# A two-block network in fp32 on one core: another order of the first loads, gated values in the temporaries' tag, mLSTM denominators by a unit column, its maxima in float32r, and a last store in two parts

## The chip, the cores and the metric

The kernel runs on one core of a Trainium2 chip, as one launch. The metric is device time in microseconds. Engines are named as in the profile: PE is TensorE's matmuls, PEld its weight loads, DVE is VectorE, ACT ScalarE, POOL GpSimd, SP the engine that issues most DMAs. A small q behind a name is that engine's sequencer.

## What is computed

A sequence of 256 rows of width 1024 goes through two blocks. The first has a SwiGLU feed-forward, a hybrid mixer (a Fourier branch and differential attention with a T5 bias by 32 distance buckets), a second SwiGLU and a norm. The second has an mLSTM mixer, a SwiGLU, causal attention with rotary positions (one block of 256, so no selected blocks), and a SwiGLU. Cut to what matters:

```python
def swiglu(x, wg, wu, wd):
    return (jax.nn.silu(x @ wg) * (x @ wu)) @ wd
...
# mLSTM, in chunks of 64, carried state c, n, m
m_t = jnp.maximum(inter, jnp.max(dmat, axis=-1))
w_intra = jnp.exp(dmat - m_t[..., None])
qk = jnp.einsum('bhtd,bhsd->bhts', qc, kc) * w_intra
num = jnp.einsum('bhts,bhsv->bhtv', qk, vc) + w_inter[..., None] * jnp.einsum('bhvd,bhtd->bhtv', c_st, qc)
den = jnp.sum(qk, axis=-1) + w_inter * jnp.einsum('bhd,bhtd->bht', n_st, qc)
h_out = num / jnp.maximum(jnp.abs(den), jnp.exp(-m_t))[..., None]
```

All weights and activations are fp32.

## The kernel before

**Pieces.** All large products run through one routine, `products`. Weights are cut into pieces of 128 x 1024 (512 KB): two row blocks of 128 by 512 columns. There are 376 pieces, laid out in the order of use by `make_plan`. A piece is split into a high part in float32r (`whi`, cast by ScalarE, L173) and the remainder (`wlo`, subtracted by VectorE, L236); activations are split in the same way. Each piece then takes 12 matmuls of 128 x 512: high weights by high and by low activations (L450, L451) and low weights by high activations (L448), into two PSUM banks, one for each half of the 256 rows. In this text pieces are counted from 0; a chunk is the pieces that add into one pair of banks. The first feed-forward (44 pieces up, 11 chunks of 4) takes its first three chunks interleaved, so pieces 0 to 11 are chunks 0 to 2 and end with pieces 9, 10 and 11; chunk 3 is pieces 12 to 15 and chunk 4 pieces 16 to 19. In the last piece of a chunk the low weights come after four matmuls, otherwise after eight.

**Order.** The schedule is written out by hand. `products` gives a piece's matmuls and then calls `step`. `step` runs what was put down for this step ahead of the pump (`pre`), the pump, what was put down for after it (`post`), and then at most a few background jobs, for which each step earns a credit. The pump of step s issues the load of piece s + 9 on SP (L159), the ScalarE cast of piece s + 4 and the VectorE remainder of piece s + 3. There are six raw buffers, six for `whi` and six for `wlo`: the load of piece k needs the remainder of piece k - 6 to be done, and the cast of piece k the matmuls of piece k - 6. Every engine works through its own instructions in order, SP through its loads too; a load also waits for the landing of one issued eight loads before.

**The start.** `start` issues the small constants on ScalarE's queue and all else on SP: the transposed input in four pairs of blocks (`xt`, 256 KB each), pieces 0 to 3, tables, and the four tiles of x (256 KB each). It splits pieces 0 to 2 itself. The rest of the constants (762 KB with gains and biases, `pos` 130 KB, tables 320 KB, gates 32 KB) is issued in `run` at step 3 (L1188 to L1191).

**A chunk's evacuation in a feed-forward** (`ffn`). One step after a chunk's last piece, `evac` writes silu(gate) with ScalarE (L501) and multiplies the other half in with VectorE (L502), in a tile with the tag g (four buffers). `turn_far` transposes it in blocks (L329), writes it to DRAM a step later (L338), reads it back turned three steps later (L335), and five steps later `split_far` splits it (L347, L348). The tile g, its transposed copy and the tile read back all have the tag g.

**Background jobs** (`t5_jobs`). They make the T5 bias during the first feed-forward: prepare (from `pos`, L517 to L521), distance, sides, least (four values into the bias and the first two values by ScalarE, L549), and then 30 copies: each has ScalarE write the two values for the next copy and VectorE copy two values into the bias where a bucket's mask holds (L564). The temporaries have the tag t2 (five buffers). The earliest place of prepare is the end of step 9; that of least is the end of step 15.

**The mLSTM** (`mlstm`). For 256 rows the recurrence is done in one piece for each of the four heads. `gates2b` scans the running maximum `mr` (4 x 256). `decay(h)` broadcasts head h's row of it over 128 partitions by a matmul with a selector, in fp32 (L881, K = 4), and makes the weights. `score(h)` multiplies the scores in (L892, L893). `numer(h)` multiplies by v (L909) and, for the denominator, by a column of ones (L911), both in fp32, where one matmul runs as two passes in the trace; it does so for the first half of rows with one product and for the second with two. ScalarE copies the result out and squares it (L913, L915). After the last numerator the output gate's sigmoid needs a table load (L794), then VectorE gates head 0 (L935) and TensorE transposes it (L308).

**The end.** `residual` adds the last sums to x and stores each 128 x 512 tile from SP (L473, L477).

Of the kernel before, what the change touches and what calls it, by code (L numbers as in the profile page):

```python
# [12 lines left out]
F32 = mybir.dt.float32  # L13
F32R = mybir.dt.float32r
# [8 lines left out]
P = 128  # L23
S = 256
D = 1024
KB = D // P
# [64 lines left out]
class Net:  # L91
# [89 lines left out]
    def start(self):  # L181

        nc, a = self.nc, self.a
        raw = [self.raw(i) for i in range(4)]
        xt = [self.slot() for _ in range(KB // 2)]

        def part(q, i, c0=0, c1=1024):
            o = self.plan[i][2]
            q.dma_start(raw[i][:, c0:c1], self.plan[i][1][:, o + c0:o + c1])

        def load_xt(q, i):
            q.dma_start(xt[i].rearrange("p (b t) -> p b t", b=2), a["xt"][2 * i:2 * i + 2].rearrange("b p t -> p b t"))

        nc.scalar.dma_start(self.cst[:, :C_AG], a["cst"][:, :C_AG])
        load_xt(nc.sync, 0)
        part(nc.sync, 0, 0, 512)
        part(nc.sync, 0, 512)
        part(nc.sync, 1)
        part(nc.sync, 2)
        load_xt(nc.sync, 1)  # L200
        part(nc.sync, 3)
        load_xt(nc.sync, 2)
        load_xt(nc.sync, 3)
        nc.sync.dma_start(self.tbl[:, :T_CMASK], a["tbl"][:, :T_CMASK])
        for c in range(2):
            for tb in range(2):
                nc.sync.dma_start(self.x[c][tb], a["x"][tb * P:(tb + 1) * P, c * 512:(c + 1) * 512])
        self.loaded = 4
# [18 lines left out]
        self.cast = 3  # L227
        for n in range(2, KB):
            self.later(max(0, n // 2 - 2), lambda n=n: split_x(n)(), post=n > 3)
# [235 lines left out]
    def residual(self, st, scale=None, gain=None, out=None):  # L465
# [3 lines left out]
        def f(c, acc):  # L469
            for tb in range(2):  # L470
# [5 lines left out]
                if out is not None:  # L476
                    nc.sync.dma_start(out[tb * P:(tb + 1) * P, c * 512:(c + 1) * 512], x)  # L477
            if st is not None and gain is None:
                self.norm_half(st, c, self.x[c])
            elif st is not None:  # L480
# [12 lines left out]
    def ffn(self, st, up, dn, res, slack=(0.0, 0.0), cross=(2, 2)):  # L493
# [3 lines left out]
        def evac(f, acc):  # L497
            ht = self.tp.tile([P, 2, S], F32, name="g", tag="g", bufs=4)
# [12 lines left out]
    def t5_jobs(self):  # L511
# [22 lines left out]
        def sides():  # L534
# [5 lines left out]
            self.bias = self.cp.tile([P, 4, 2 * S], F32, name="t5bias")  # L540

        def least():
            for h in range(4):
                value(0, h, self.bias[:, h])
            lay(1, 0)
# [11 lines left out]
        def copy(b, i):  # L557
# [5 lines left out]
            for j in range(2):  # L563
                nc.vector.copy_predicated(self.bias[:, 2 * i + j], T["m"], v[j])  # L564
# [204 lines left out]
    def mlstm(self, st, res):  # L769
# [7 lines left out]
        sel = self.slot()  # L777
# [526 lines left out]
```

## Time and profile before

| | |
|---|---|
| median of 3 runs | 1111.71 us (1111.59 to 1113.0) |
| the profiled execution's own time | 1112.17 us |
| its span, first to last instruction | 1110.4 us |
| busy: PE, PEld, DVE, ACT | 99%, 82%, 66%, 56% |
| bytes moved by DMA | 226 MB, 204 GB/s in the mean |
| granted TensorE clock, mean | 1.00 |

How to read it: the time is that of the profiled run, the span what the trace covers. Matmuls are pipelined, so PE's busy share says that matmuls follow each other, not that each runs at its peak; a lost microsecond is seen where the start of a matmul is late, not in the share. The rows further below are from that one execution.

### The profile page before, as it was taken

The page shows a single profiled execution, that of the slowest core. Times are in us where ns is not written, and L with a number is a line of the kernel's source. Part 1 is how long each engine was busy: PE and PEld are TensorE (multiplying, and loading weights), DVE is VectorE, ACT ScalarE, POOL GpSimd, SP SyncE. Part 2 cuts the span into 40 slices and gives each one's busy share as a digit, 9 for nine tenths or more (in the row PEclk, how much of TensorE's full clock was granted, in tenths as well). Part 3 has the DMA queues.
Part 4 walks back from the last instruction along what each step waited for, and adds up shares of the span by engine and source line. Part 5 has one row for each costly group of instructions (what it writes and reads, how often), then busy time and mean ns, then how long its engine had stood idle before and what let it go on. Part 6 is the DMA issues. An engine that isn't in the chain of part 4 may idle for free.

```text
span 1110.4 us, 14227 instructions
## 1 busy us (share of the span) xinstructions
PE 1099.4 (99%) x5034; PEld 909.2 (82%) x5034; DVE 727.7 (66%) x1136; ACT 620.2 (56%) x927; POOL 24.6 (2%) x27
## 2 busy tenths in 40 slices
PE   8999999999999999999999999999999999999998
PEld 7878888878888888888877888888888888888887
DVE  5689998475685665645654677756558865665752
ACT  6497876666645554535645564545445665554541
POOL 0000000000000000000001000000003000000000
PEclk9999999999999999999999999999999999999999
DMA  9788876543555877766443556877455445777760
GB/s 319 271 242 245 256 237 205 190 151 112 193 173 166 255 230 258 225 210 209 155 130 113 191 187 212 282 251 268 156 173 180 147 151 182 245 233 247 241 229 29
DMA packets 89583, 226.19 MB, mean 204 GB/s; under 512 B 10148, under 2 KB 34340, under 8 KB 89512
## 3 DMA queue, kind: packets, MB, share of 16 engines
q1 hardware_dynamic: 88928, 224.86, 62.7%
q8 instruction: 39, 0.64, 0.2%
q10 hardware_dynamic: 584, 0.44, 0.2%
q14 instruction: 32, 0.26, 0.1%
HBM read 212.67 MB, written 12.58 MB: 203 GB/s over the span
## 4 chain that ended last, share of the span: by engine, by line
PE 94%; DMA 2%; DVE 2%; ACT 1%; issue 1%; SPq 1%; DVEq 0%; ACTq 0%
PE acc L450 29%; PE acc L448 29%; PE acc L451 29%; DMA wraw<-f_up 2%; PE acc L308 2%; DVE wlo L236 1%; PE acc L909 1%; PE acc L616 0%; PE acc L661 0%; SPq L335 0%; PE acc L1053 0%; PE acc L702 0%; PE acc L1079 0%; PE acc L1111 0%; DVE g L502 0%
## 5 line engine op out<-in xcount | busy, mean ns | idle before, releaser
L236 DVE TENSOR_TENSOR wlo<-wraw,whi 128x1024 fp32r<-128x1024 f32 x373 | 441.2, 1214 | 47.8 <-ACT whi L173 47.6
L173 ACT ACTIVATE whi<-wraw 128x1024 fp32r<-128x1024 f32 x373 | 381.2, 1053 | 108.6 <-PE acc L451 76.8
L450 PE MATMUL acc<-whi,xs 128*128 128x512 f32 x1024 | 404.4, 395 | 2.3 <-ACT whi L224 1.4
L451 PE MATMUL acc<-whi,xs 128*128 128x512 f32 x1024 | 399.0, 390 | 0.0
L448 PE MATMUL acc<-wlo,xs 128*128 128x512 f32 x1024 | 284.7, 389 | 2.7 <-DVE wlo L236 2.7
L450 PEld LDWEIGHTS acc<-whi,xs 128*128 128x128 f32 x1024 | 192.2, 188 | 44.6 <-issue 2.7
L448 PEld LDWEIGHTS acc<-wlo,xs 128*128 128x128 f32 x1024 | 192.1, 188 | 43.8 <-DVE wlo L236 3.6
L451 PEld LDWEIGHTS acc<-whi,xs 128*128 128x128 f32 x1024 | 192.4, 188 | 38.7
L450 PE MATMUL acc<-whi,h 128*128 128x512 f32 x480 | 187.9, 391 | 0.0
L451 PE MATMUL acc<-whi,h 128*128 128x512 f32 x480 | 186.8, 389 | 0.0
L448 PE MATMUL acc<-wlo,h 128*128 128x512 f32 x480 | 131.3, 389 | 0.0
L502 DVE SCALAR_TENSOR_TENSOR g<-acc,rsqn,g 128x256 f32<-128x256 f32 x88 | 40.9, 480 | 112.1 <-ACT g L501 111.4
L448 PEld LDWEIGHTS acc<-wlo,h 128*128 128x128 f32 x480 | 90.1, 188 | 18.8
L451 PEld LDWEIGHTS acc<-whi,h 128*128 128x128 f32 x480 | 90.2, 188 | 18.4
L450 PEld LDWEIGHTS acc<-whi,h 128*128 128x128 f32 x480 | 90.1, 188 | 18.3
L501 ACT ACTIVATE g<-acc,rsqn 128x256 f32<-128x256 f32 x88 | 39.8, 471 | 110.1 <-PE acc L448 109.3
L347 ACT ACTIVATE h<-g 128x512 fp32r<-128x512 f32 x44 | 27.6, 628 | 47.6 <-DMA g<-far 47.4
L292 ACT ACTIVATE xs<-acc,cst 128x256 fp32r<-128x256 f32 x48 | 21.5, 473 | 56.2 <-PE acc L308 42.7
L348 DVE TENSOR_TENSOR h<-g,h 128x512 fp32r<-128x512 f32 x44 | 30.2, 686 | 31.1 <-ACT h L347 31.1
L549 ACT ACTIVATE t<-side,cst 128x512 f32<-128x512 bf16 x60 | 45.4, 802 | 1.6 <-DVE t5bias L564 1.6
L473 DVE TENSOR_TENSOR x<-acc,x 128x512 f32<-128x512 f32 x20 | 13.5, 688 | 45.7 <-PE acc L448 45.7
L564 DVE COPY_PREDICATED t5bias<-t5m,t 128x512 f32<-128x512 uint8 x60 | 41.3, 743 | 0.5
(222 smaller groups left out, 525.5 us busy)
## 6 DMA issues: line engine op xcount, KB each, us to landing
wraw<-g_up SPq DMA_DIRECT2D x88, 512.0 KB, 5.0
wraw<-f_up SPq DMA_DIRECT2D x87, 512.0 KB, 5.3
wraw<-f_dn SPq DMA_DIRECT2D x44, 512.0 KB, 4.3
wraw<-g_dn SPq DMA_DIRECT2D x44, 512.0 KB, 4.4
wraw<-w_in SPq DMA_DIRECT2D x32, 512.0 KB, 4.1
wraw<-a_w_in SPq DMA_DIRECT2D x24, 512.0 KB, 4.5
wraw<-b_w_in SPq DMA_DIRECT2D x24, 512.0 KB, 4.8
far<-g SPq DMA_DIRECT2D x44, 256.0 KB, 4.4
```

Source lines behind the costliest of these rows:

```text
L173: nc.scalar.activation(wh[:, :m], raw[:, :m], AF.Copy)
L236: self.nc.vector.tensor_sub(wl[:, :m], raw[:, :m], self.pieces[i][1][:, :m].bitcast(F32))
L308: self.nc.tensor.transpose(pt[:, o:o + P], src[tb][:, j * P:(j + 1) * P], self.ident)
L347: nc.scalar.activation(to(hi), src, AF.Copy)
L348: nc.vector.tensor_sub(to(lo), src, to(hi).bitcast(F32))
L448: nc.tensor.matmul(acc[tb], xh, w[kk][1], start=False, stop=last and kk == 1)
L450: nc.tensor.matmul(acc[tb], xh, w[kk][0], start=k == 0, stop=False)
L451: nc.tensor.matmul(acc[tb], xl, w[kk][0], start=False, stop=False)
L501: nc.scalar.activation(ht[:, tb], acc[tb][:, :S], AF.Silu, scale=r)
L502: nc.vector.scalar_tensor_tensor(ht[:, tb], acc[tb][:, S:], r, ht[:, tb], ALU.mult, ALU.mult)
L549: nc.scalar.activation(dst, T["side"], AF.Identity, bias=self.cst[:, c:c + 1], scale=self.cst[:, c + 64:c + 65])
L564: nc.vector.copy_predicated(self.bias[:, 2 * i + j], T["m"], v[j])
```

## The change

It does five things. `start` issues the loads in another order: eight constants and the first block of the transposed input on ScalarE's queue; on SP the first half of piece 0, the second block, and then pieces 0 to 5 with the other blocks between, then x tiles alternating with pieces 6 to 8, and the constants behind them. The warm-up matmuls follow the loads in the program and are nine instead of ten. The splits of the other blocks, the squares of x, the norm and the rest of the constants move to later steps (the constants from step 3 to step 6). The gated tile in `ffn` takes its buffer from the tag t2 instead of g. In the mLSTM, v lies in the T5 bias's memory (free by then, 257 wide for each head), with a column of ones, so that the numerator's matmul gives the denominator in column 256; the running maxima are split in two float32r halves and broadcast by two float32r matmuls. The last tile is added and stored in two halves, the second from ScalarE's queue.

```diff
 
     def start(self):
...
         nc, a = self.nc, self.a
-        raw = [self.raw(i) for i in range(4)]
+        raw = {}
         xt = [self.slot() for _ in range(KB // 2)]
 
-        def part(q, i, c0=0, c1=1024):
+        def part(i, c0=0, c1=1024):
+            if i not in raw:
+                raw[i] = self.raw(i)
             o = self.plan[i][2]
-            q.dma_start(raw[i][:, c0:c1], self.plan[i][1][:, o + c0:o + c1])
-
-        def load_xt(q, i):
-            q.dma_start(xt[i].rearrange("p (b t) -> p b t", b=2), a["xt"][2 * i:2 * i + 2].rearrange("b p t -> p b t"))
-
-        nc.scalar.dma_start(self.cst[:, :C_AG], a["cst"][:, :C_AG])
-        load_xt(nc.sync, 0)
-        part(nc.sync, 0, 0, 512)
-        part(nc.sync, 0, 512)
-        part(nc.sync, 1)
-        part(nc.sync, 2)
+            nc.sync.dma_start(raw[i][:, c0:c1], self.plan[i][1][:, o + c0:o + c1])
+            self.loaded = i + 1
+
+        def load_xt(q, n, m=1):
+            o = n % 2 * S
+            q.dma_start(xt[n // 2][:, o:o + m * S].rearrange("p (b t) -> p b t", b=m),
+                        a["xt"][n:n + m].rearrange("b p t -> p b t"))
+
+        def load_x(c, tb):
+            nc.sync.dma_start(self.x[c][tb], a["x"][tb * P:(tb + 1) * P, c * 512:(c + 1) * 512])
+
+        nc.scalar.dma_start(self.cst[:, :KB], a["cst"][:, :KB])
+        load_xt(nc.scalar, 0)
+        part(0, 0, 512)
         load_xt(nc.sync, 1)
-        part(nc.sync, 3)
-        load_xt(nc.sync, 2)
-        load_xt(nc.sync, 3)
-        nc.sync.dma_start(self.tbl[:, :T_CMASK], a["tbl"][:, :T_CMASK])
-        for c in range(2):
-            for tb in range(2):
-                nc.sync.dma_start(self.x[c][tb], a["x"][tb * P:(tb + 1) * P, c * 512:(c + 1) * 512])
-        self.loaded = 4
+        part(0, 512)
+        part(1)
+        part(2)
+        load_xt(nc.sync, 2, 2)
+        part(3)
+        part(4)
+        load_xt(nc.sync, 4, 2)
+        part(5)
+        load_xt(nc.sync, 6, 2)
+        load_x(0, 0)
+
+        z = self.tmp("sq")
+        nc.vector.memset(z, 0.0)
+        nc.scalar.activation(self.tmp("sq")[:, :8], z[:, :8], AF.Copy)
+        junk = self.bank()
+        for _ in range(9):
+            nc.tensor.matmul(junk[:, :P], z[:, :P], z[:, P:], start=True, stop=True)
         xs = [self.xsp.tile([P, 2, S], F32R, name="xs", tag="xs") for _ in range(KB)]
 
         def split_x(n):
                 lo()
                 nc.vector.tensor_sub(w[1][:, c], raw[i][:, c], w[0][:, c].bitcast(F32))
         self.cast = 3
+        for i, c, tb in ((6, 0, 1), (7, 1, 0), (8, 1, 1)):
+            part(i)
+            load_x(c, tb)
+        nc.sync.dma_start(self.cst[:, KB:C_AG], a["cst"][:, KB:C_AG])
+        nc.sync.dma_start(self.tbl[:, :T_CMASK], a["tbl"][:, :T_CMASK])
         for n in range(2, KB):
-            self.later(max(0, n // 2 - 2), lambda n=n: split_x(n)(), post=n > 3)
+            self.later(n // 2 * 2 - 2, lambda n=n: split_x(n)(), post=True)
         return [(t[:, 0], t[:, 1]) for t in xs]
...
                 self.later(1, lambda c=c, acc=accs.pop(c): evac(c, acc))
             self.step(slack if at >= skip else 0.0)
 
-    def residual(self, st, scale=None, gain=None, out=None):
+    def store(self, out):
+
+        nc = self.nc
+
+        def f(c, acc):
+            for tb in range(2):
+                x = self.x[c][tb]
+                n = 2 if c and tb else 1
+                for i in range(n):
+                    s = slice(i * S, (i + 1) * S) if n == 2 else slice(0, 512)
+                    nc.vector.tensor_add(x[:, s], acc[tb][:, s], x[:, s])
+                    q = nc.scalar if i else nc.sync
+                    q.dma_start(out[tb * P:(tb + 1) * P, c * 512 + s.start:c * 512 + s.stop], x[:, s])
+
+        return f
...
         hs = []
 
         def evac(f, acc):
-            ht = self.tp.tile([P, 2, S], F32, name="g", tag="g", bufs=4)
+            ht = self.tmp2().rearrange("p (t c) -> p t c", t=2)
             for tb in range(2):
                 r = st["rc"][:, tb:tb + 1]
                 nc.scalar.activation(ht[:, tb], acc[tb][:, :S], AF.Silu, scale=r)
...
-            self.bias = self.cp.tile([P, 4, 2 * S], F32, name="t5bias")
+            self.bias = self.cp.tile([P, 4, 2 * (S + 1)], F32, name="t5bias")
...
             for j in range(2):
-                nc.vector.copy_predicated(self.bias[:, 2 * i + j], T["m"], v[j])
+                nc.vector.copy_predicated(self.bias[:, 2 * i + j, :2 * S], T["m"], v[j])
...
         v, so = {}, {}
         G = {}
         rc = lambda tb: st["rc"][:, tb:tb + 1]
-        sel = self.slot()
+        sel, selr = self.slot(), self.hp.tile([P, 512], F32R, name="h", tag="h")
         nc.scalar.dma_start(sel[:H], self.a["tbl"][:H, T_SEL:T_SEL + 512])
+        self.later(3, lambda: nc.vector.tensor_copy(selr[:H], sel[:H]))
...
 
         def ev_v(g, acc):
             for tb in range(2):
-                v[g, tb] = self.slot()
-                nc.scalar.activation(v[g, tb], acc[tb], AF.Copy, scale=rc(tb))
+                v[g, tb] = self.bias[:, 2 * g + tb].rearrange("p (h d) -> p h d", h=2)
+                nc.gpsimd.memset(v[g, tb][:, :, S:], 1.0)
+                nc.scalar.activation(v[g, tb][:, :, :S], acc[tb].rearrange("p (h d) -> p h d", h=2), AF.Copy, scale=rc(tb))
...
             pt = self.aux()
             for tb in range(2):
                 nc.tensor.transpose(pt[:H, tb * P:(tb + 1) * P], ac[:, tb], self.ident)
-            ar = self.sp.tile([H, S], F32, name="gar", tag="gar", bufs=1)
+            ar = self.tmp("sq")[:H]
             mr = self.sp.tile([H, S], F32, name="gmr", tag="gmr", bufs=1)
             nc.vector.tensor_copy(ar, pt[:H, :S])
             nc.vector.tensor_tensor_scan(mr, ar, ar, 0.0, ALU.max, ALU.max)
-            G["mr"] = mr
+            both = self.hp.tile([P, 2, S], F32R, name="h", tag="h")
+            mh, ml = both[:H, 0], both[:H, 1]
+            nc.vector.tensor_copy(mh, mr)
+            nc.vector.tensor_sub(ml, mr, mh.bitcast(F32))
+            G.update(mr=mr, mhl=(mh, ml))
...
         def decay(h):
             ac = G["ac"]
             pw = self.aux()
-            nc.tensor.matmul(pw[:, :S], sel[:H, h * P:(h + 1) * P], G["mr"], start=True, stop=True)
+            for i in range(2):
+                nc.tensor.matmul(pw[:, :S], selr[:H, h * P:(h + 1) * P], G["mhl"][i], start=i == 0, stop=i == 1)
             wt = self.slot()[:, :384]
...
             dens[h], sums[h] = self.col("adn", 2), self.col("ass", 2)
             for tb in range(2):
                 pn = self.aux()
-                c = slice((h % 2) * S, (h % 2 + 1) * S)
-                vs = [(v[h // 2, 0][:, c], pr[:, tb * P:(tb + 1) * P])]
+                vs = [(v[h // 2, 0][:, h % 2], pr[:, tb * P:(tb + 1) * P])]
                 if tb:
-                    vs.append((v[h // 2, 1][:, c], pr[:, S:384]))
+                    vs.append((v[h // 2, 1][:, h % 2], pr[:, S:384]))
                 for i, (vv, pp) in enumerate(vs):
-                    nc.tensor.matmul(pn[:, :S], pp, vv, start=i == 0, stop=i == tb)
-                for i, (vv, pp) in enumerate(vs):
-                    nc.tensor.matmul(pn[:, S:S + 1], pp, self.one[:, 0:1], start=i == 0, stop=i == tb)
+                    nc.tensor.matmul(pn[:, :S + 1], pp, vv, start=i == 0, stop=i == tb)
                 n = num[h][:, tb * S:(tb + 1) * S]
                 nc.scalar.activation(n, pn[:, :S], AF.Copy)
                 nc.vector.tensor_copy(dens[h][:, tb:tb + 1], pn[:, S:S + 1])
...
         nc.gpsimd.memset(self.mhalf, -0.5)
-
-        z = self.tmp("sq")
-        nc.vector.memset(z, 0.0)
-        nc.scalar.activation(self.tmp("sq")[:, :8], z[:, :8], AF.Copy)
-        junk = self.bank()
-        for _ in range(10):
-            nc.tensor.matmul(junk[:, :P], z[:, :P], z[:, P:], start=True, stop=True)
         st = self.norm_new("ffn1_norm")
         st["xs"] = self.start()
         for c in range(2):
             for tb in range(2):
-                self.later(3 + 2 * c + tb, lambda c=c, tb=tb: self.square(
+                self.later(5 + 2 * c + tb, lambda c=c, tb=tb: self.square(
                     self.x[c][tb], st["ss"][:, 2 * c + tb:2 * c + tb + 1]), post=True)
-        self.norm_end(st, 7)
+        self.norm_end(st, 8)
 
...
-        self.later(3, constants, post=True)
+        self.later(6, constants, post=True)
...
-        self.ffn(nx, "g1_up", "g1_dn", self.residual(None, out=a["out"]))
+        self.ffn(nx, "g1_up", "g1_dn", self.store(a["out"]))
```

## Rows read from the trace of the kernel before

**Rows 1.** The page, busy time of each engine: busy us, share of the span, instructions.
```profile
PE 1099.4 (99%) x5034; PEld 909.2 (82%) x5034; DVE 727.7 (66%) x1136; ACT 620.2 (56%) x927; POOL 24.6 (2%) x27
```

**Rows 2.** The waits of PE over the whole run: who waited for whom, us in total, times, longest.
```profile
PE acc L448 <- DVE wlo L236: 2.7, 2, 2.4
...
PE acc L450 <- ACT whi L224: 1.4, 1, 1.4
```

**Rows 3.** The timeline of all engines at the start: start us, duration us, engine, line, operation, out<-in, count, and in brackets the idle time before it and what ended it.
```profile
8.48 1.06 ACT L224 ACTIVATE whi<-wraw 128x1024 fp32r<-128x1024 f32 x1 [1.96 <-DMA wraw<-f_up]
...
9.59 0.50 PE L450 MATMUL acc<-whi,xs 128*128 128x512 f32 x1 [1.37 <-ACT whi L224]
...
9.80 1.06 ACT L224 ACTIVATE whi<-wraw 128x1024 fp32r<-128x1024 f32 x1 [0.26 <-DMA wraw<-f_up]
...
11.85 11.85 SPq L159 DMA_DIRECT2D wraw<-f_up  x8
...
17.86 1.06 ACT L173 ACTIVATE whi<-wraw 128x1024 fp32r<-128x1024 f32 x1 [4.95 <-DMA wraw<-f_up]
...
18.97 0.50 PE L450 MATMUL acc<-whi,xs 128*128 128x512 f32 x1 [0.92 <-ACT whi L173]
```

**Rows 4.** The timeline of PE, the first matmul of piece 5 and that of piece 7.
```profile
22.46 0.39 PE L450 MATMUL acc<-whi,xs 128*128 128x512 f32 x1
...
27.91 0.39 PE L450 MATMUL acc<-whi,xs 128*128 128x512 f32 x1
```

**Rows 5.** Three stretches: us, busy time (and instructions) of PE, PEld, DVE, ACT, POOL, the granted clock, the DMA share and GB/s.
```profile
10.00:22.00 12.00, 10.74 (x46) 8.22 (x45) 6.68 (x10) 6.85 (x11) 0.00 (x0) 1.00 1.04 399
...
22.00:30.00 8.00, 8.00 (x37) 6.62 (x36) 7.37 (x10) 7.72 (x14) 0.26 (x1) 1.00 0.88 277
...
61.00:125.00 64.00, 61.63 (x272) 50.73 (x271) 62.28 (x87) 53.47 (x75) 0.00 (x0) 1.00 0.82 248
```

**Rows 6.** The timelines of ACT, DVE, SP and PE between 33 and 64 us, in order of time.
```profile
33.73 0.30 DVE L517 TENSOR_SCALAR t<-pos 128x258 int32<-128x258 int32 x1
...
34.35 0.28 DVE L521 CAST t<-t 128x258 f32<-128x258 int32 x1
...
36.08 1.06 ACT L173 ACTIVATE whi<-wraw 128x1024 fp32r<-128x1024 f32 x1 [3.70 <-DMA wraw<-f_up]
...
37.16 1.28 ACT L501 ACT_TABLE_LOAD   x1
...
38.97 0.88 DVE L502 SCALAR_TENSOR_TENSOR g<-acc,rsqn,g 128x256 f32<-128x256 f32 x2 [4.33 <-ACT g L501]
...
49.43 3.68 SPq L335 DMA_DIRECT2D g<-far  x4
...
55.94 0.63 ACT L347 ACTIVATE h<-g 128x512 fp32r<-128x512 f32 x1 [8.50 <-DMA g<-far]
...
60.71 0.81 ACT L501 ACTIVATE g<-acc,rsqn 128x256 f32<-128x256 f32 x2
...
62.74 1.18 DVE L236 TENSOR_TENSOR wlo<-wraw,whi 128x1024 fp32r<-128x1024 f32 x1
...
63.98 0.50 PE L448 MATMUL acc<-wlo,xs 128*128 128x512 f32 x1 [2.37 <-DVE wlo L236]
```

**Rows 7.** The bias jobs: the page's group of ScalarE's values over the whole run (busy us, mean ns), VectorE's group of copies in the stretch 61 to 125, and from the waits of the stretch 60 to 190 those of ScalarE's values.
```profile
L549 ACT ACTIVATE t<-side,cst 128x512 f32<-128x512 bf16 x60 | 45.4, 802 | 1.6 <-DVE t5bias L564 1.6
...
L564 DVE COPY_PREDICATED t5bias<-t5m,t 128x512 f32<-128x512 uint8 x28 | 19.3, 743 | 0.2
...
ACT t L549 <- DVE t5bias L564: 1.6, 2, 1.0
```

**Rows 8.** The timeline of PE, the numerator of head 0 and the first score matmul behind it.
```profile
577.66 0.59 PE L909 MATMUL acc<-h 128*128 128x256 f32 x2
578.09 0.28 PE L911 MATMUL acc<-tbl,h 128*128 128x1 f32 x2
578.23 1.11 PE L909 MATMUL acc<-h 128*128 128x256 f32 x4
579.18 0.50 PE L911 MATMUL acc<-tbl,h 128*128 128x1 f32 x4
579.54 0.46 PE L892 MATMUL acc<-h 128*128 128x256 f32 x1
```

**Rows 9.** The timeline of PE: the 16 float32r matmuls of the gates and what follows, and the broadcast of the maxima of one head and what follows.
```profile
540.83 2.01 PE L812 MATMUL acc<-xs,gs 128*16 128x256 f32 x16
542.67 0.40 PE L450 MATMUL acc<-whi,xs 128*128 128x512 f32 x1
...
574.18 0.69 PE L881 MATMUL acc<-gmr,h 4*128 4x256 f32 x2
574.81 0.50 PE L450 MATMUL acc<-whi,xs 128*128 128x512 f32 x1
```

**Rows 10.** The timelines of ACT and PE behind the last numerator.
```profile
601.42 0.38 ACT L913 ACTIVATE h<-acc 128x256 f32<-128x256 f32 x1 [0.33 <-PE acc L911]
...
604.92 0.33 PE L308 MATMUL acc<-tbl,h 128*128 128x128 f32 x1 [0.68 <-DVE h L935]
```

**Rows 11.** The end: the last addition in the timeline of DVE, and the last store in the DMA view (KB, us from issue to landing).
```profile
1106.57 0.69 DVE L473 TENSOR_TENSOR x<-acc,x 128x512 f32<-128x512 f32 x1 [0.67 <-PE acc L448]
...
out<-x SPq DMA_DIRECT2D x1, 256.0 KB, 2.0
```

More of the change, by code (lines that the diff above doesn't have):

```diff
@@ L463, in products, with residual @@
             self.step(slack if at >= skip else 0.0)
-    def residual(self, st, scale=None, gain=None, out=None):
+    def store(self, out):
[10 more added lines that the diff above has]
+        return f
+    def residual(self, st, scale=None, gain=None):
         nc = self.nc
@@ L475, in f @@
                     nc.vector.scalar_tensor_tensor(x, acc[tb], scale, x, ALU.mult, ALU.add)
-                if out is not None:
-                    nc.sync.dma_start(out[tb * P:(tb + 1) * P, c * 512:(c + 1) * 512], x)
-            if st is not None and gain is None:
+            if gain is None:
                 self.norm_half(st, c, self.x[c])
-            elif st is not None:
+            else:
                 new = [self.xp.tile([P, 512], F32, name="x", tag="x") for _ in range(2)]
@@ L539, in sides @@
             nc.vector.tensor_sub(c, c, self.cst[:, C_REL:C_REL + 64])
-            self.bias = self.cp.tile([P, 4, 2 * S], F32, name="t5bias")
+            self.bias = self.cp.tile([P, 4, 2 * (S + 1)], F32, name="t5bias")
         def least():
             for h in range(4):
-                value(0, h, self.bias[:, h])
+                value(0, h, self.bias[:, h, :2 * S])
             lay(1, 0)
```

## The prediction

> **What bounds the kernel now.** I read the page first: the span is 1110.4 us and TensorE is busy for 99% of it [rows 1]. One piece of weights (512 KB, 12 matmuls) takes 2.72 us of TensorE: two of them lie between 22.46 and 27.91 [rows 4]. So only two things shorten the run: less TensorE work, or a stretch in which TensorE waits. The second view is therefore TensorE's waits. The reader is to see how few there are [rows 2]: a few in the first 22 us and one of 2.4 us for a low-order half (wlo); the timeline adds one ahead of the mLSTM's output [rows 10]. The third view is the timeline of those places.
>
> The start. Piece 1's raw data land at 8.48, and its matmuls start at 9.59. Piece 4's load is issued at 11.85 only, behind the four x loads, and lands at 17.86; piece 4 starts at 18.97, and piece 5 at 22.46 [rows 3, 4]. Without waits, pieces 1 to 4 would need 4 x 2.72 = 10.88 us, and piece 5 would start at 20.47. So 2.0 us are lost behind piece 1.
>
> The wait at 61. TensorE idles 2.37 us before 63.98, for piece 19's wlo, which VectorE starts at 62.74 [rows 6]. Backwards: that stands in order behind the evacuation of chunk 3 (ScalarE 60.71), behind six bias values of 0.8 us and the split at 55.94, which waited for the turned tile's read. That read was issued at 49.43, behind piece 21's load, which needs piece 15's raw buffer and so VectorE's work from 38.97 on, dense up to there. 38.97 is the first evacuation; on ScalarE it stood behind piece 13's cast, which waited for its data until 36.08, and a table load [rows 6]. From 38.97 to the end of that wlo it is 25 us of one chain, whose steps depend on each other and not on TensorE.
>
> **The change, part by part.**
>
> *Load order.* Up to piece 1, SP sends the same bytes in the same slots (first half, one x block, second half, piece 1); ScalarE's queue takes the small constants and the other x block. I leave piece 1 at 8.48 and its first matmul at 9.59. It could come 0.5 us earlier (one issue slot) or 1.0 later (half of the 1.96 us for which ScalarE waited for it [rows 3]); the later end would leave TensorE's limit, below, at just the term that I take. Piece 1 was among the first five loads issued and still kept ScalarE waiting that long, so issue is not what limits it. If the second queue did bring the data earlier after all, it would raise TensorE's limit by the 0.5 us and leave the sum, which pos sets.
>
> Behind piece 1: pieces 2, 3, 4 follow with one x^T load between them and no x rows ahead. From piece 2's landing (9.80) at the 399 GB/s of the stretch 10 to 22 [rows 3, 5], piece 3 with its x^T pair (768 KB) lands at 11.8 and piece 4 at 13.1; they are needed at 15.0 and 17.75. Casts (1.06 us on ScalarE, 1.2 on VectorE) and the splits of x^T fit between. So TensorE's own limit is a gain of 2.0 at piece 5, and 4.4 at piece 19 if the wait there goes too.
>
> What is late next? The bias job "prepare" needs pos, which the change issues at step 6 instead of 3: SP's queue then has the loads of pieces 13 to 15 ahead of it, and piece 15 waits for piece 9's raw buffer (26.4: by the count below it lands at 24.2, and both casts take 2.2). Behind the waiting prepare, VectorE has the first evacuation and piece 13's wlo queued, and SP has piece 19's load and the turned tiles' transfers. From piece 2's landing to the end of pos there are x^T 768, x 1024, pieces 3 to 15 6656, constants 28 + 192 + 762, and pos 130 KB: 9560 KB, 9.79 MB. At 399 GB/s that is 24.5 us, so pos lands at 34.3. If it runs for 8 us at the 277 GB/s of the stretch 22 to 30, in which SP had let the queue run thin, 1.0 MB more stand in line and it is 36.8 [rows 5]. I take 34.6: with x behind the weights, pieces 4 to 8 free their raw buffers some 4 us earlier, so the queue stays filled. Prepare takes 0.9 (33.73 to 34.63), so the first evacuation is on VectorE at 35.55 against 38.97 [rows 6]. ScalarE is ready: piece 13 lands by 30, the table load runs early, and piece 9's sums end at 9.59 + 9 x 2.72 = 34.1. The chain of 25 us then moves up by 3.4 us, less than TensorE's 4.4, so a wait of 1.0 us stays at piece 19 and **this part gives 3.4 us**. Bounds: 4.9 (piece 1 earlier, pos no limit) and 0.5 (pos at 37 and the turned tile's read 0.7 slower).
>
> *Gated values in t2.* It removes nothing from TensorE. The bias jobs hold two to four of the five t2 buffers by the code, and in 61 to 125 VectorE is busy for 62.3 of 64 us with wlo and 28 predicated copies [rows 5, 7]. A wait there costs directly. I take 0: with the buffers taken in turn, a gated tile gets one that was released a job earlier. Bounds: 0.3 gained (the turned tiles have the four g buffers alone) and 1.0 lost; the rival below has the worse case.
>
> *Unit column.* Per head now: two N=256 passes in 0.43, two N=1 passes 0.14, four N=256 passes 0.95, four N=1 passes 0.36, together 1.88 from 577.66 to 579.54 [rows 8]. 0.95 is 0.09 over four times 0.215, since the weight load behind the short passes is not hidden; the same 0.08 falls on what follows. After: six passes of 257 columns, 6 x 0.216 = 1.30. Saved 0.66 a head, three times 2.0 us. After the last head TensorE waits for ScalarE's chain (601.42 copy, square, table load, sigmoid, then L935, for which the first L308 starts at 604.92 only [rows 10]); this chain gets its second half 0.56 earlier, but must first finish the first half's square, which leaves 0.43. Sum **2.4 us**; bounds 1.9 (only the N=1 passes go) and 2.8. POOL's four memsets have no reader before these matmuls; the ScalarE copy into the same tile waits for them at most 0.3 us beside TensorE's stream.
>
> *Maxima in float32r.* Two fp32 passes of a K=4 matmul take 0.63 (574.18 to 574.81), 0.20 more than two with hidden loads. Two float32r passes of 256 columns take 2 x 0.115 (16 of them in 1.84 us) [rows 9] plus the same 0.20, 0.43. Saved 0.20 four times, **0.8 us**; bounds 0.4 (the loads hide worse behind shorter passes) and 1.3. The two VectorE operations that make the halves (0.4 us each, 4 partitions) lie two steps, over 5 us, ahead of their first reader; the wlo queued behind them is made three pieces ahead by the code.
>
> *Last store.* The last addition takes 0.69, and the store 2.0 from issue to landing [rows 11]. Two halves: the first is issued some 0.2 earlier, the second 0.1 to 0.2 later, but with half the bytes (0.3 to 0.5 less). I take **0.2 us**; bounds -0.2 and 0.5.
>
> *Sum:* 3.4 + 2.4 + 0.8 + 0.2 = 6.8 us. The profiled execution took 1112.17 (its span and 1.8 around it), so 1105.4; the median of the runs is 0.46 lower, so **1104.9**.
>
> **The rivals.**
>
> *A. The front gain is mostly swallowed.* Pos lands at 37 and the wait at piece 19 stays almost whole. For it: the front is DMA-bound, and the 277 GB/s came just where casts and loads meet. Against: the queue that ran thin there is fuller now. The front gives 0.9 and the sum 4.3: 1107.4.
>
> *B. Unhidden weight loads.* If each of the six wider passes paid its load, as a K=4 pass does (0.63 / 2 = 0.315 [rows 9]), they would take 1.9 and the unit column would give nothing: 6.8 - 2.4 = 4.4, so 1107.3. Against it: passes of the same shape follow each other at 0.215 today [rows 8]. The Trainium skill speaks for it in "TensorE: Matmul & The Clock Gate", section "Part 3: Packing small matmuls — row/col tiling": weight loads overlap running matmuls only when the row group differs. By that rule B is what happens; this trace disagrees for K=128, with 0.215 a pass.
>
> *C. Slower: ScalarE and VectorE take turns on t2.* If a gated tile leaves the jobs no spare buffer, a job's second value (0.8 us on ScalarE [rows 7]) waits for the copy of the job before, and VectorE idles 0.8 us a job. Fourteen jobs lie in the full stretch: 11.2 us, and VectorE has no lead to hide them, since TensorE waits for it at 63.98. Against the 6.8 us of the sum that is 4.4 slower, 1116.1. The sign turns once nine of the fourteen jobs wait (6.8 / 0.8). Against it: today two such waits, 1.6 us in all, are seen [rows 7], and evacuations come only every fourth step.
>
> *D. Nothing measurable.* A and B together, with 1 to 2 us of waits from C (6.8 - 2.5 - 2.4 - 1.5 = 0.4): 1111.3.
>
> **How the numbers follow.** The forecast (1102.5 to 1106.3) gets 0.65, A 0.16, B 0.06, C 0.07, D 0.06. About 0.2% (2.2 us) is what a measurement of this kernel can tell from no change. Faster: 0.65 + 0.16 + 0.06 = 0.87; within: 0.06; slower: 0.07. The range goes from the sum of the favourable bounds (4.9 + 2.8 + 1.3 + 0.5, cut to 9.3 because not all come together) to A with the other parts at their low bounds (0.9 + 1.9 + 0.4 - 0.2 = 3.0, and 0.3 lost on t2): 1102.4 to 1109.0.
>
> **What would show it.** Right: piece 1's cast near 8.5 and piece 5's first matmul near 20.5; prepare at 34 to 35.5 and the first evacuation on VectorE near 35.5; 0.5 to 1.5 us of waiting at piece 19; six passes at 0.216 in each numerator; 0.43 per maximum; the same wait before the first L308 behind the mLSTM. Wrong: prepare beyond 37 (A), passes of 0.3 (B), VectorE idle behind ScalarE between 61 and 125 with predicated copies as the cause (C), or a new wait of TensorE anywhere else.

## The result and the profile after

| | before | changed |
|---|---|---|
| median, us | 1112.0 (1111.59 to 1113.0, 4 runs) | 1104.8 (1103.92 to 1106.53, 4 runs) |
| ratio, 95% interval | | 0.9931 [0.9918, 0.9945] |
| profiled execution, us | 1112.17 | 1104.58 |
| its span, us | 1110.4 | 1102.8 |
| first matmul of piece 5 | 22.46 | 19.79 |
| first VectorE evacuation | 38.97 | 35.27 |
| low half of piece 19 on TensorE | 63.98 | 59.68 |
| first transposes of x, behind the first 512 columns of the first feed-forward's sums | 163.85 | 159.55 |
| from the gates' matmuls to the first matmul behind the mLSTM | 64.09 | 60.69 |
| from the last matmul's start to the end of the span | 4.24 | 4.04 |

The kernel is faster by 0.7%; 1104.9 was predicted. The first thing read of the changed kernel is the page: the busy time of the engines, against [rows 1].

```profile
PE 1095.1 (99%) x5008; PEld 906.3 (82%) x5008; DVE 729.0 (66%) x1140; ACT 621.1 (56%) x927; POOL 24.7 (2%) x31
```

4.3 of the 7.6 us of span are TensorE work; the rest is waiting that has gone. TensorE's waits over the whole run, against [rows 2] (who waited for whom, us, times, longest):

```profile
PE acc L328 <- DVE h L973: 1.1, 2, 0.8
PE acc L470 <- ACT whi L239: 1.0, 1, 1.0
PE acc L468 <- DVE wlo L256: 0.7, 1, 0.7
```

The wait for wlo at piece 19 is down from 2.4 to 0.7 and not gone. The timeline of the start, against [rows 3, 4]:

```profile
4.87 0.51 ACT L312 ACTIVATE xs<-h,cst 128x256 fp32r<-128x256 f32 x1 [1.71 <-DMA h<-xt]
...
5.95 0.50 PE L470 MATMUL acc<-whi,xs 128*128 128x512 f32 x1 [1.03 <-ACT whi L239]
...
7.13 1.06 ACT L239 ACTIVATE whi<-wraw 128x1024 fp32r<-128x1024 f32 x1 [0.32 <-DMA wraw<-f_up]
...
8.80 0.39 PE L470 MATMUL acc<-whi,xs 128*128 128x512 f32 x1
...
19.79 0.39 PE L470 MATMUL acc<-whi,xs 128*128 128x512 f32 x1
```

Piece 0 starts 0.74 us later (5.95 in place of 5.21), since ScalarE waits for the x^T block on its own queue. Piece 1's data are there 1.35 us earlier (7.13, in [rows 3] 8.48), and from 5.95 to the wait at piece 19 TensorE has no gap. The timelines of VectorE, SP, ScalarE and TensorE around the wait at piece 19, against [rows 6]:

```profile
34.45 0.30 DVE L551 TENSOR_SCALAR t<-pos 128x258 int32<-128x258 int32 x1 [1.92 <-DMA pos<-pos]
...
35.27 0.88 DVE L536 SCALAR_TENSOR_TENSOR t<-acc,rsqn,t 128x256 f32<-128x256 f32 x2
...
45.74 1.81 SPq L355 DMA_DIRECT2D g<-far  x4
...
51.63 0.63 ACT L367 ACTIVATE h<-g 128x512 fp32r<-128x512 f32 x1 [6.96 <-DMA g<-far]
...
58.44 1.18 DVE L256 TENSOR_TENSOR wlo<-wraw,whi 128x1024 fp32r<-128x1024 f32 x1
...
59.68 0.73 PE L468 MATMUL acc<-wlo,xs 128*128 128x512 f32 x2 [0.74 <-DVE wlo L256]
```

VectorE waits 1.92 us for pos, and the first evacuation follows the last of prepare's four operations at once. The mLSTM on TensorE, against [rows 8 to 10]: a maximum, a numerator, and what follows the last one.

```profile
565.58 0.50 PE L922 MATMUL acc<-h 4*128 4x256 f32 x2
566.01 0.50 PE L470 MATMUL acc<-whi,xs 128*128 128x512 f32 x1
...
572.84 1.46 PE L949 MATMUL acc<-t5bias,h 128*128 128x257 f32 x6
574.13 0.59 PE L933 MATMUL acc<-h 128*128 128x256 f32 x2
...
592.34 1.46 PE L949 MATMUL acc<-t5bias,h 128*128 128x257 f32 x6
...
597.35 0.33 PE L328 MATMUL acc<-tbl,h 128*128 128x128 f32 x1 [0.80 <-DVE h L973]
```

A maximum takes 0.43 us in place of 0.63, six passes 1.29 (0.215 each) in place of 1.88. The stores at the end in the DMA view (KB, us to landing), against [rows 11]:

```profile
out<-x SPq DMA_DIRECT2D x1, 128.0 KB, 1.8
out<-x ACTq DMA_DIRECT2D x1, 128.0 KB, 1.9
```

### The profile page after: what moved, and what is told of

Read it like the earlier page. It is cut to its first block, busy times and chain, and to the rows that moved or that the text cites. A ratio compares the mean times of both kernels' runs of the same rounds, so it can differ in the third digit from the quotient of the medians.

```text
span 1102.8 us, 14184 instructions
## 1 busy us (share of the span) xinstructions
PE 1095.1 (99%) x5008; PEld 906.3 (82%) x5008; DVE 729.0 (66%) x1140; ACT 621.1 (56%) x927; POOL 24.7 (2%) x31
## 4 chain that ended last, share of the span: by engine, by line
PE 94%; DMA 3%; DVE 1%; ACT 1%; SPq 0%; issue 0%; DVEq 0%; ACTq 0%
PE acc L470 29%; PE acc L468 29%; PE acc L471 29%; PE acc L328 2%; DMA wraw<-f_up 1%; DMA g<-far 1%; DVE wlo L256 1%; DMA pos<-pos 1%; PE acc L949 0%; PE acc L650 0%; PE acc L695 0%; PE acc L1091 0%; PE acc L736 0%; PE acc L1117 0%; PE acc L1149 0%; DMA cst<-cst 0%
## 5 line engine op out<-in xcount | busy, mean ns | idle before, releaser
L536 DVE SCALAR_TENSOR_TENSOR t<-acc,rsqn,t 128x256 f32<-128x256 f32 x88 | 41.0, 482 | 105.1 <-ACT t L535 105.1
L535 ACT ACTIVATE t<-acc,rsqn 128x256 f32<-128x256 f32 x88 | 40.2, 471 | 108.6 <-PE acc L468 108.6
L367 ACT ACTIVATE h<-g 128x512 fp32r<-128x512 f32 x44 | 27.7, 629 | 53.8 <-DMA g<-far 53.8
L319 DVE SCALAR_TENSOR_TENSOR xs<-acc,cst,xs 128x256 fp32r<-128x256 f32 x48 | 22.1, 482 | 25.6 <-ACT xs L312 25.6
```

The source lines that it names most:

```text
L319: nc.vector.scalar_tensor_tensor(dst[:, 1], src, gain, dst[:, 0].bitcast(F32), ALU.mult, ALU.subtract)
L367: nc.scalar.activation(to(hi), src, AF.Copy)
L535: nc.scalar.activation(ht[:, tb], acc[tb][:, :S], AF.Silu, scale=r)
L536: nc.vector.scalar_tensor_tensor(ht[:, tb], acc[tb][:, S:], r, ht[:, tb], ALU.mult, ALU.mult)
```

## The experiments

The theory: 4.3 us are the load order's, 3.4 the mLSTM's, 0.1 to 0.2 the store's, nothing the tag's. Twelve kernels ran, in three sets; the kernel before ran beside each set, with medians of 1112.71 (`front_only`, `unit_only`, `max_only`, `t2_back`), 1113.86 (`store_whole`, `pos_early`, `xt0_on_sp`, `pos_and_xt0`) and 1112.01 (the four others). Ratios are against the one of the same set. Those medians differ by 1.9 us, so ratios of different sets compare to no better than 0.2%. In nine of the twelve the profiled execution took longer than the median of its kernel, by up to 2.2 us. So a part is sized by distances inside the traces, and the time stands beside them.

### One part at a time

`front_only` is the kernel before with the new `start` alone, of which these are the main lines (and the steps 5 to 8, 8 and 6 for squares, row sums and constants):

```diff
+        nc.scalar.dma_start(self.cst[:, :KB], a["cst"][:, :KB])
+        load_xt(nc.scalar, 0)
+        part(0, 0, 512)
...
-        for _ in range(10):
+        for _ in range(9):
```

> The kernel before with the load order alone (the start, its warm-up and the steps of the squares, the row sums and the constants). Theory: all that TensorE gained up to 61 us in the changed kernel (4.3 us) is the load order's; the profiled time falls by 4.3 us against before, TensorE's wait at piece 19 is 0.9 us, and the first VectorE evacuation is at 35.3. Rival: 0.6 us of the 4.3 came from the gated values' move to t2, which leaves the g buffers to the turned tiles (their read took 5.8 us from issue in the changed kernel, 6.5 before); then this kernel gains 3.7, and waits 1.5 us at piece 19.

Measured: 1107.75, ratio 0.9959 [0.9945, 0.9973], by which it is 4.6 us less. The profiled time missed the expectation: it fell by 2.3 us, not 4.3. VectorE's first evacuation is at 35.88, the waits show 0.6 us at piece 19, and piece 20 starts at 63.26, 2.7 us earlier than before. So the load order brings the large part without the tag. What took the rest from this trace is seen in TensorE's timeline behind the warm-up:

```profile
5.95 0.79 PE L470 MATMUL acc<-whi,xs 128*128 128x512 f32 x1 [0.55 <-ACT whi L239]
6.54 0.63 PE L471 MATMUL acc<-whi,xs 128*128 128x512 f32 x1
6.96 0.63 PE L470 MATMUL acc<-whi,xs 128*128 128x512 f32 x1
7.39 0.63 PE L471 MATMUL acc<-whi,xs 128*128 128x512 f32 x1
```

The matmuls follow each other at 0.43 us, not 0.23, up to 10.2. So piece 5 starts at 21.59 there, and the span (1108.1) is no measure of the part. The wait at piece 19 can't tell the theory from its rival either, since TensorE comes later to it.

`unit_only` and `max_only` are the kernel before with one part each; their main lines:

```diff
+                v[g, tb] = self.bias[:, 2 * g + tb].rearrange("p (h d) -> p h d", h=2)
+                nc.gpsimd.memset(v[g, tb][:, :, S:], 1.0)
...
+                    nc.tensor.matmul(pn[:, :S + 1], pp, vv, start=i == 0, stop=i == tb)
```

```diff
-            nc.tensor.matmul(pw[:, :S], sel[:H, h * P:(h + 1) * P], G["mr"], start=True, stop=True)
+            for i in range(2):
+                nc.tensor.matmul(pw[:, :S], selr[:H, h * P:(h + 1) * P], G["mhl"][i], start=i == 0, stop=i == 1)
```

> The kernel before with the unit column alone (values in the bias tile with a column of ones, six passes of 257 columns a head). Theory: 2.5 us faster: 0.65 us in each of the first three heads, 0.55 between the last numerator's first pass and the first matmul on the normalized rows (5.56 us before, 5.01 in the changed kernel). Rival: passes that pay for their weight loads, 0.3 us each, and no gain.

> The kernel before with the maxima in float32r alone. Theory: each of the four broadcasts takes TensorE 0.43 us in place of 0.63, 0.8 us faster in all. Rival: the two VectorE operations that make the halves and the copy of the selector delay a low-order half of the weights, and up to 0.8 us of the gain comes back as a wait for wlo between 540 and 575 us.

Measured: 1110.67, ratio 0.9981 [0.9969, 0.9992], and 1111.75, ratio 0.9996 [0.9984, 1.0007]. (One of the twelve runs of `unit_only` took 6365.89 us; it is not in the ratio, and no trace shows what held it.) In TensorE's timeline the stretch from the gates' matmuls to the first matmul behind the mLSTM tells it more sharply. First the kernel with the unit column, then the one with the maxima:

```profile
541.52 2.00 PE L813 MATMUL acc<-xs,gs 128*16 128x256 f32 x16
...
603.08 0.33 PE L308 MATMUL acc<-tbl,h 128*128 128x128 f32 x1 [0.80 <-DVE h L933]
```

```profile
540.30 2.01 PE L813 MATMUL acc<-xs,gs 128*16 128x256 f32 x16
...
603.53 0.33 PE L308 MATMUL acc<-tbl,h 128*128 128x128 f32 x1 [0.68 <-DVE h L941]
```

61.56 and 63.23 us against 64.09 [rows 9, 10]: 2.53 and 0.86, together 3.39, and with both parts it is 3.40. Both rivals fall: six wider passes pay no weight load, and no wlo comes late between 540 and 575. The time of the maxima alone can't be told from nothing; that of the column can.

`store_whole` is the changed kernel with the last store whole:

```diff
-                n = 2 if c and tb else 1
+                n = 1
```

> The changed kernel with the last store in one part again. Theory: from the last matmul's start to the store's last landing it takes 3.40 us in place of 3.32, 0.1 to 0.2 us slower, which five rounds can hardly tell from nothing. Rival: the second queue was worth more or less than nothing, 0.5 us either way.

Measured: 1105.82, ratio 0.9931 [0.9912, 0.9950], which is the changed kernel's ratio in the first comparison. From the last matmul's start to the end of the span it takes 4.17, with two parts 4.03 to 4.04 in all nine traces that have them: 0.1 us. Half a microsecond either way, the rival, is not seen in that stretch.

### The tag of the gated values

`t2_back`:

```diff
-            ht = self.tmp2().rearrange("p (t c) -> p t c", t=2)
+            ht = self.tp.tile([P, 2, S], F32, name="g", tag="g", bufs=4)
```

> The changed kernel with the gated values back in the tag g. Theory: no difference in time within 0.5 us; VectorE's wlo in 61 to 125 us come as far ahead of TensorE as before (1.8 us for pieces 35 and 39, 3.0 for 43) in place of 0.5 to 1.0. Rival 1: the turned tile's read is later by 0.6 us and TensorE waits 1.5 us at piece 19 in place of 0.9: 0.6 us slower. Rival 2: the tag t2 costs waits that its gain elsewhere hides, and this kernel is 0.5 us or more faster.

Measured: 1106.0, ratio 0.9937 [0.9923, 0.9951]. The low halves of pieces 35, 39 and 43 come 1.2, 1.3 and 0.5 us ahead of TensorE, not the 1.8, 1.8 and 3.0 that were expected. The trace has a wait at piece 19 of 1.3 us and new ones at 161, behind the additions of the first feed-forward's first 512 columns (L511). In TensorE's waits:

```profile
PE acc L328 <- DVE x L511: 1.6, 2, 1.3
PE acc L468 <- DVE wlo L256: 1.3, 1, 1.3
```

That looked like the tag's price, so the pair was run again later with an earlier pos (below): `warm12_pos` with t2, `warm12_pos_g` with g.

> As the last, with the gated values back in tag g. Theory: the same time within 0.5 us, no wait of TensorE at 160 us. Rival (the tag does matter): with g shared by gated and turned tiles VectorE comes to the first block's additions 1 to 2 us later, as in the trace of the changed kernel with tag g, TensorE waits at the transposes behind them (1.4 and 0.5 us there), and this kernel is 0.5 to 2 us slower.

Measured: 1103.95 with g (ratio 0.9925 [0.9911, 0.9940]), 1104.85 with t2 (0.9933 [0.9919, 0.9947]). From piece 20 to the transposes behind those additions it takes 98.87 us with g and 98.76 with t2, and both kernels wait 0.9 us there, where no wait was expected. So that wait isn't the tag's, and the rival falls: the tag is worth nothing that shows here. The wait is for VectorE, whose timeline in `warm12_pos` is dense with predicated copies up to the additions:

```profile
158.41 1.35 DVE L598 COPY_PREDICATED t5bias<-t5m,t 128x512 f32<-128x512 uint8 x2
159.67 1.26 DVE L511 SCALAR_TENSOR_TENSOR x<-acc,x 128x512 f32<-128x512 f32 x2
```

TensorE's last matmul ahead of it starts at 159.36. But the copies alone don't make VectorE late. In the first trace of the changed kernel TensorE starts piece 20 at the same 61.62, VectorE has the same copies, and its additions come 1.58 us earlier:

```profile
158.09 1.28 DVE L511 SCALAR_TENSOR_TENSOR x<-acc,x 128x512 f32<-128x512 f32 x2
```

TensorE doesn't wait there. The difference is in the turned tiles: between 61 and 162 us VectorE waits 3.0 us for ScalarE to split them in that trace, and 4.5, 4.3 and 4.8 in `warm12_pos`, `warm12_pos_g` and `t2_back`. One of them in the timelines of ScalarE and VectorE in `warm12_pos`:

```profile
146.78 0.63 ACT L367 ACTIVATE h<-g 128x512 fp32r<-128x512 f32 x1 [2.80 <-DMA g<-far]
...
147.44 0.69 DVE L368 TENSOR_TENSOR h<-g,h 128x512 fp32r<-128x512 f32 x1 [1.23 <-ACT h L367]
```

So VectorE is nearly the bound in this stretch, and reads that land late make it the bound. That a sooner start of TensorE gains no more there is not shown.

### What sets the wait at piece 19

`pos_early`, `xt0_on_sp`, and `pos_and_xt0` with both edits:

```diff
-            nc.sync.dma_start(self.pos, a["pos"])
...
+        self.later(3, lambda: nc.sync.dma_start(self.pos, a["pos"]), post=True)
```

```diff
-        load_xt(nc.scalar, 0)
+        load_xt(nc.sync, 0)
```

> The changed kernel with the load of pos alone moved from step 6 back to step 3; the other constants stay at step 6. Theory: the landing of pos (34.4 us) holds the first VectorE evacuation (35.3), and through a chain of 24.4 us the low-order half of piece 19; with pos some 6 us earlier the evacuation is free from about 33 on, when ScalarE and TensorE have its accumulator, the wait of 0.9 us at piece 19 goes, and the kernel is 0.9 us faster. Rival: another link of the chain, the turned tile's read or piece 13's data, sets the wait, and the time stays within 0.3 us.

> The changed kernel with the first x^T block back at the head of SP's queue; ScalarE's queue keeps the small constants alone. Theory: the first matmul of piece 0 comes at 5.2 as in the kernel before, in place of 5.95, since the block no longer waits on ScalarE's queue; piece 1's data land a slot later, at 7.6 to 8.5 in place of 7.1, so piece 1 starts at 8.7 to 9.6 (8.80 now). The time stays within 0.3 us, since pos sets the wait at piece 19 in either case. Rival: TensorE's stream starts 0.7 us earlier and everything behind it moves up, 0.7 us faster.

> Both: pos at step 3 and the first x^T block at the head of SP's queue. Theory: with pos out of the way the earlier start counts: 0.9 us of pos and up to 0.7 us of the start, 0.9 to 1.6 us faster than the changed kernel. Rival: piece 1's data then land at 8.5, TensorE's stream is set by them as before (piece 5 at 20.5), and no more than 0.2 to 0.9 us are gained.

Measured: 1105.16 (0.9930 [0.9913, 0.9948]), 1106.86 (0.9944 [0.9926, 0.9963]), 1105.21 (0.9931 [0.9915, 0.9948]). All three intervals hold the changed kernel's 0.9931, so neither a gain nor a loss against it is seen in the time; it did not run in this set itself. The trace of `pos_early` has the matmuls at 0.43 us as well, up to 10.0, and so its first evacuation comes at 35.99: it settles nothing, and `warm12_pos` below has its edit with a longer warm-up. In `xt0_on_sp` piece 1 missed what was expected by more than a slot. The timelines of ScalarE and TensorE, piece 1's cast and first matmul:

```profile
9.28 1.06 ACT L239 ACTIVATE whi<-wraw 128x1024 fp32r<-128x1024 f32 x1 [2.26 <-DMA wraw<-f_up]
...
10.39 0.50 PE L470 MATMUL acc<-whi,xs 128*128 128x512 f32 x1 [1.66 <-ACT whi L239]
```

Piece 0 starts at 4.97, a microsecond earlier, but piece 1's cast comes 2.15 us later than in the first trace of the changed kernel (7.13), and piece 5 1.6 later, at 21.40; `pos_and_xt0` repeats it (9.02, 10.12 and 21.31). In all nine traces with the block on ScalarE's queue the cast lies between 7.13 and 7.90. So the block's place on the other queue is what brings piece 1 early, by 1.1 to 2.2 us. One issue slot is 0.47 of that; what the rest is, no run shows.

`changed_again` is the changed kernel; `warm12` has this edit, and `warm12_pos` this one and pos at step 3:

```diff
-        for _ in range(9):
+        for _ in range(12):
```

> The changed kernel itself once more, as the base of this call and for a second trace of its start. Piece 0 starts at 5.7 to 6.0 us, up to a microsecond behind the last of 9 warm-up passes. Theory (clock): in some executions TensorE's first matmuls of 512 columns take 0.43 us in place of 0.23, as in the traces of the load order alone and of pos early (ten of them, 2.0 us), so the runs spread over more than 2 us; and the wait at piece 19 lies between 0.9 and 2.4 us, because the turned tile's read takes 5.8 to 7.4 us from its issue, with the same code. Rival: both were chance of those two kernels' code, and this trace looks like the first one (0.23 us, 0.9 us of waiting).

> The changed kernel with 12 warm-up matmuls in place of 9, so that they end at 5.6 us and not at 4.6 to 5.0. Theory (clock): no trace has matmuls of 0.43 us behind the warm-up; piece 1 starts at 8.8; the slow executions disappear, 0.3 to 0.7 us in the median against the changed kernel of this call. Rival: the pause has nothing to do with it, or the three passes delay piece 0, and the median is the same or 0.3 us worse.

> 12 warm-up matmuls and pos at step 3. Theory (pos sets the wait): piece 5 starts at 19.8, the first VectorE evacuation follows TensorE by 14.3 us, at 34.1 in place of 35.3, the turned tile is taken 16.4 to 17.7 us later, at 50.5 to 51.8, and piece 19's low half comes 8.04 us behind that: a wait of 0 to 1.3 us where the changed kernel has 0.9 to 2.4, and 1.0 to 1.2 us less than with 12 warm-up matmuls alone. Rival: the turned tile's read, queued behind weights, lands no earlier than 52 in any case, and nothing is gained.

Measured: 1105.81 (0.9946 [0.9931, 0.9960]), 1105.78 (0.9945 [0.9931, 0.9959]), 1104.85 (0.9933 [0.9919, 0.9947]). The expectation of the longer warm-up fell: the median is the same to 0.03 us. `changed_again`, the same code, shows another trace than the first. Timelines of SP and ScalarE, then of TensorE:

```profile
45.78 1.81 SPq L355 DMA_DIRECT2D g<-far  x4
...
53.44 0.63 ACT L367 ACTIVATE h<-g 128x512 fp32r<-128x512 f32 x1 [8.61 <-DMA g<-far]
...
61.48 0.73 PE L468 MATMUL acc<-wlo,xs 128*128 128x512 f32 x2 [2.39 <-DVE wlo L256]
```

The evacuation (35.32) and the read's issue stand within 0.05 us of where they stood, but the read takes 7.7 us from issue to use in place of 5.9, and the wait is 2.39. In `warm12_pos` the 12 passes end late, piece 0 starts at 6.32 and piece 5 at 20.38, not at 19.8. The step that pos decides comes at the expected distance from there:

```profile
31.86 0.29 DVE L551 TENSOR_SCALAR t<-pos 128x258 int32<-128x258 int32 x1
...
34.69 0.88 DVE L536 SCALAR_TENSOR_TENSOR t<-acc,rsqn,t 128x256 f32<-128x256 f32 x2 [1.94 <-ACT t L535]
...
51.61 0.63 ACT L367 ACTIVATE h<-g 128x512 fp32r<-128x512 f32 x1 [6.34 <-DMA g<-far]
```

TensorE's start now sets the evacuation, 14.3 us behind piece 5. But the turned tile is taken (ScalarE's split, L367) at 51.61 here and at 51.86 with g, where the evacuation was at 33.83. Over the eleven traces with the new order it is 16.4 to 18.1 us from the first evacuation to the take of that tile, and from the take to piece 19's low half 8.04 or 8.05 in the ten in which TensorE waits there. So both are true: in the two traces of the changed kernel pos held the evacuation back by 1.2 and 1.1 us (35.27 and 35.32, against 14.3 behind piece 5 at 19.79 and 19.94), and the read behind it has 1.8 us of scatter of its own. In the time that is about 1 us: 1104.85, and 1103.95 with g, against 1105.81 of the changed kernel in the same set. Four of five runs of either lie below all five of the changed kernel, but the ratios' intervals overlap.

## Why the prediction was right, and where its steps were not

*The sum* was 6.8 us. By the ratios it was 7.6 (0.9931) in the first comparison and 6.0 (0.9946) in `changed_again`. In the first pair of traces the stretches give 4.3 up to the transposes at 160, 3.4 in the mLSTM and 0.2 at the end; TensorE's other stretches are 0.3 longer. That the median came within 0.1 us of the forecast is partly luck: the same code had 1105.81 later, and the largest term, the load order's, varies by more from trace to trace.

*Load order, 3.4.* The mechanism held: x behind the weights, pos as the next limit (landed 34.4, taken as 34.6), evacuation at 35.27 (35.55), a wait left at piece 19. The size was wrong in being one number. "The chain of 25 us" was 24.4 us in the first trace of the changed kernel, 25.8 in `store_whole`, whose code is the same up to there, and 26.2 in `changed_again`. The three traces begin piece 20 at 61.62, 63.21 and 63.88, against 65.93 before, 65.92 in `unit_only` and 65.41 in `max_only`: 1.5 to 4.3 us earlier, 2.9 in the mean, and the forecast lies inside. The prediction's lower bound of 0.5 doesn't follow from its own terms: pos at 37 puts the evacuation at 37.95, 1.0 earlier than before, and 0.7 off that leaves 0.3. The range was made with 0.9 and doesn't change.

*"I leave piece 1 at 8.48"* is the step that failed. In the first trace the cast came at 7.13 and the first matmul at 8.80, not 9.59 (7.82 and 8.93 in `changed_again`). As the prediction put it, that raised TensorE's own limit (2.67 in place of 2.0 at piece 5, though piece 0 started 0.74 later) and left the sum to pos. Its premise, "the same bytes in the same slots", was wrong: up to piece 1 SP had sent a pair of x^T blocks (256 KB) and now sends one (128 KB). `xt0_on_sp`, which gives SP that block back, shows that this is the cause, and that it is worth more than the 0.5 us of an issue slot.

*Unit column, 2.4*: 2.53, by `unit_only`; behind the last head 0.55 in place of 0.43. The Trainium skill ("TensorE: Matmul & The Clock Gate", section "Part 3: Packing small matmuls — row/col tiling") lets weight loads overlap running matmuls only where the row group differs; by that rule it would have been nothing. The traces disagree: the six passes of 257 columns take 0.215 each, and no run shows them at 0.3. *Maxima, 0.8*: 0.86, 0.43 each as worked out. *Last store, 0.2*: 0.1, by `store_whole`. *Gated values, 0*: 0, by the pair.

*The rivals.* A needed pos at 37; it landed at 34.4, and at the latest of the traces at 36.3 (`xt0_on_sp`). Its other half, a wait at piece 19 that stays almost whole, did come in two of the three traces of this code (2.39 and 2.29 us), by the scatter of the read behind pos. B fell with `unit_only`. C fell: ScalarE's values wait 1.4 us for copies over the whole run, as before (1.6). VectorE was closer to TensorE in the first trace (half a microsecond of lead at pieces 35 and 39, 1.8 before), but not in `store_whole` (1.9 at both). D fell with A and B.

## What to carry to other kernels

When a wait goes, look at the next engine that is nearly full: here VectorE comes to the additions at 160 us about when TensorE does, and in three traces late reads made TensorE wait there, which no view of TensorE's waits showed before. A single small load moved off the queue that feeds the first weights can be worth more than its own bytes: 128 KB moved piece 1 by 1.1 to 2.2 us, though the run's time doesn't show that clear of noise. Read the same code's second trace before a microsecond of a DMA-bound stretch is put down to an edit.

## What the runs showed of the hardware

A wait of TensorE may cost more than itself. In `changed_again` the wait of 2.39 us was followed by matmuls at 0.43 us. Its stretches (us, busy time and instructions of PE, PEld, DVE, ACT, POOL, the granted clock, DMA share, GB/s):

```profile
61.00:63.00 2.00, 1.52 (x6) 1.24 (x7) 2.00 (x3) 2.00 (x4) 0.00 (x0) 0.98 0.10 12
63.00:66.00 3.00, 3.00 (x8) 2.31 (x7) 2.96 (x6) 3.00 (x5) 0.00 (x0) 0.50 0.84 233
```

The granted clock is 0.50 from 63 to 66, the lower level of 1.2 GHz; about seven matmuls at 0.2 us more cost 1.5 us. In the kernel before the wait of 2.37 us left it at 1.00, and so did that of 2.29 us in `store_whole`. The runs carry their mean granted clock: 0.998 or less in 29 of 66 runs with the old start (before, `unit_only`, `max_only`), and in 3 of 56 with the new one. Runs of before with it took 1114.1 in the mean, the others 1111.4. By these numbers about 1 us of the load order's gain (an estimate: 2.6 x 29/66) is clock, which no term of the sum had. Where the clock fell in the runs without a trace is not shown, and so neither is that it was the wait at piece 19.

At the start the lower level shows in the matmuls alone. In `front_only` the stretch has ten matmuls where the changed kernel has 19, at 0.427 us for 512 columns, which is 1.2 GHz, though the column says 1.00:

```profile
5.90:10.20 4.30, 4.25 (x10) 3.36 (x11) 2.90 (x4) 2.95 (x4) 0.00 (x0) 1.00 0.97 346
```

The warm-up passes went from 0.21 to 0.11 us each as early as behind the 13th, and in `warm12_pos` not before its end, so the number of passes that does is not fixed. In two traces of six with nine warm-up matmuls and the block on ScalarE's queue, piece 0 then ran slow, 2.0 us; in the other four it didn't, though TensorE had paused 0.61 to 1.03 us ahead of it there, and 0.55 and 0.65 in those two. What decides it is open, and the runs with 12 were not faster.
